# Unsplit float32 expert weights in column strips of the array, with wider transfers and a reordered gather and scatter

## The chip, the cores and the metric

The kernel runs on one core of a Trainium2 chip. The metric is the device time of one execution in microseconds. The kernel before takes 2220.1 us (median of 3 runs, 2218.81 to 2220.77); a difference of 0.2% is about what a measurement of it can tell from none.

A core has a matrix engine (TensorE, PE in the profile; its stationary operand is loaded by separate instructions, PEld), a vector engine (VectorE, DVE), a scalar engine (ScalarE, ACT), GpSimd (POOL) and a queue engine (SyncE, SP) that here does nothing but issue transfers from the chip's main memory.

## The reference

256 tokens of width 1024 pass through two layers of a three-branch mixer, each followed by a feed-forward part (a dense one in the first layer, a mixture of experts in the second), and then through two attention blocks ("fox" and "dsw"). All of it is float32. The change concerns the mixture of experts:

```python
def _moe(h, router_w, router_b, w1, w3, w2):
    logits = (h @ router_w).astype(f32) + router_b.astype(f32)
    probs = jax.nn.softmax(logits, axis=-1)
    top_p, top_i = lax.top_k(probs, TOP_K)                 # 2 of 8 experts per token
    top_p = top_p / jnp.sum(top_p, axis=-1, keepdims=True)
    combine = jnp.sum(jax.nn.one_hot(top_i, N_EXPERTS) * top_p[..., None], axis=-2)
    out = jnp.zeros_like(h)
    for e in range(N_EXPERTS):
        out = out + combine[..., e:e + 1] * _swiglu(h, w1[e], w3[e], w2[e])
    return out                                             # _swiglu: (silu(h @ w1) * (h @ w3)) @ w2
```

w1 and w3 of an expert are 1024 x 2816, w2 is 2816 x 1024. The eight experts' weights are 8 x 3 x 1024 x 2816 x 4 bytes = 276.8 MB, and each is read once. With the inputs given, the router sends 94, 51, 81, 60, 46, 61, 59 and 60 tokens to the experts 0 to 7.

## The kernel before

**How the order is made.** Nearly all instructions are recorded (`Recorder.add`, which is why the profile gives line 95 for them) and put in order by a list scheduler (`Recorder.flush`): it simulates five engines with estimated durations, and picks for each the ready operation of the highest priority. A transfer counts there with its bytes over 360. A `join()` keeps a group of matmuls together as one operation. Transfers go into tiles of fixed pools (`TAGS`: name, bytes per partition, count), and each is issued on SP in that order, so a transfer waits until its tile's last reader is done, and all behind it wait as well. There are two recorded programs: everything up to the end of the experts, and the two attention blocks. Between them the kernel reads the count of the fullest expert, and runs `experts` a second time if some expert has more places than one pass holds.

**The experts (`moe`, `experts`).** Each token gets a place in its expert's list, of which a pass holds 128. A 0/1 matrix G per pair of experts picks the tokens' rows (the gather, 256 columns for the two experts). The normalised tokens are held as a rounded part and a remainder (`s.th`, `s.tl`) in the type float32r, which the array takes in one pass where float32 takes two at half the column rate; the gathered X therefore also has two parts. A weight arrives as float32 in chunks of 512 columns (`chunk`, tag `raw`, 1 MB: four row tiles of 128 x 512). ScalarE copies each 128 x 1024 piece to float32r (`wh`), VectorE subtracts that from the raw piece (`wl`), and `mm3` multiplies three ways: high x high, high x low, low x high, each with the 128 places as stationary operand and 512 columns of weights streaming. w1 and w3 take 8 row tiles per chunk, and their chunks are 5 x 512 and 256 columns. The product g is transposed in 128 x 128 blocks (`turn`), split as well, and multiplied by w2 (`down`): 22 row tiles of two times 512 columns. Per expert that is 8 x 5 x 2 x 3 + 22 x 2 x 3 = 372 matmuls of 512 columns and 8 x 2 x 3 = 48 of 256.

**The scatter.** After two experts the outputs, times the combine weight and the modulation gate, are split and multiplied by the transposed G: 16 matmuls of 512 columns per pair.

**Names in the rows.** `pa`, `pb`, `pt` are PSUM tiles (3, 4 and 1 banks); `F`, `Y`, `G` hold gathered tokens (printed without their digit), `P` the transposed g, `T` scratch, `E` the 0/1 matrices, `hh` and `hl` parts of activations, `M` two more tiles for split weights.

Of the kernel before, what the change touches and what calls it, by code (L numbers as in the profile page):

```python
# [58 lines left out]
class Recorder:  # L59
# [9 lines left out]
    def reset(s):  # L69
        s.ops, s.hist, s.bias, s.wait, s.joined = [], {}, 0.0, WAIT, None  # L70
# [14 lines left out]
    @contextmanager  # L85
    def join(s):

        s.joined = []
        yield
        s.joined = None  # L90

    def add(s, engine, method, args, kw):
# [81 lines left out]
    def flush(s, hold=()):  # L174
# [70 lines left out]
        while events:  # L245
# [9 lines left out]
            while again:  # L255
                again = False
                for e in engines:
# [94 lines left out]
class Net:  # L352
# [166 lines left out]
    def chunk(s, src, mode, tags=None):  # L519
# [35 lines left out]
        return get  # L555

# [762 lines left out]
    def moe(s):  # L1319
# [60 lines left out]
        s.slots = s.c([128, 128], name="slots")  # L1380
        nc.gpsimd.iota(s.slots, pattern=[[1, 128]], base=0, channel_multiplier=0, allow_small_or_imprecise_dtypes=True)
# [10 lines left out]
        s.raws = itertools.chain(["raw"] * 5 + ["Y4"] * 4 + ["hh", "hl"], itertools.repeat("raw"))  # L1392
        s.wh, s.wl = itertools.cycle(["wh"] * 4 + ["M4"]), itertools.cycle(["wl"] * 4 + ["M4"])
        s.experts(0)
        s.wh, s.wl = itertools.repeat("wh"), itertools.repeat("wl")
# [3 lines left out]
        with s.tc.If(vals[0] > 128):  # L1399
            s.experts(128)  # L1400
        s.nc = s.rec

    def experts(s, base):

        nc, A = s.nc, s.A
        for e in range(8):
            if e % 2 == 0 and e and base == 0:
                s.raws = itertools.chain(["raw"] * 8, ["hh", "hl"], itertools.repeat("raw"))
            if e % 2 == 0:

                G = [s.t([128, 2, 128], "E2", F32R) for _ in range(2)]
                for b in range(2):
                    for i in range(2):
                        pos = s.pos[:, b, e + i:e + i + 1]
                        if base:
                            q = s.t([128, 1], "sa")
                            nc.vector.tensor_scalar(q, pos, float(base), None, ALU.subtract)
                            pos = q
                        nc.vector.tensor_scalar(G[b][:, i], s.slots, pos, s.self[:, b, e + i:e + i + 1],
                                                ALU.is_equal, ALU.mult)  # L1420
                tag = ("Y4",) * 4 if e % 4 == 2 else ("F4", "F4", "G4", "G4")
                X = [s.t([128, 4, 256], z, F32R) for z in tag]
                for k2 in range(0, 8, 2):
                    for i, th in enumerate((s.th, s.tl)):
                        p = s.ps("pa", (128, 2, 256))
                        for k in range(2):
                            f = (k2 + k) * 128
                            for b in range(2):
                                nc.tensor.matmul(p[:, k], th[b][:, f:f + 128], G[b].rearrange("p i t -> p (i t)"),
                                                 start=b == 0, stop=b == 1)  # L1430
                        nc.scalar.activation(X[2 * i + k2 // 4][:, k2 % 4:k2 % 4 + 2], p, AF.Copy)

                GTs, cws = [], []
                for i in range(2):
                    p = s.ps("pt")
                    for b in range(2):
                        nc.tensor.transpose(p[:, b * 128:b * 128 + 128], G[b][:, i].bitcast(F32), s.ident)
                    for b in range(2):
                        nc.tensor.matmul(p[:, 256:264], G[b][:, i].bitcast(F32), s.comb[:, b], start=b == 0, stop=b == 1)
                    GT, cw = s.t([128, 256], "E2", F32R), s.t([128, 1], "sa")  # L1440
                    nc.scalar.activation(GT, p[:, 0:256], AF.Copy)
                    nc.vector.tensor_copy(cw, p[:, 256 + e + i:257 + e + i])
                    GTs.append(GT)
                    cws.append(cw)
            o = e % 2 * 128
            xk = lambda k: (X[k // 4][:, k % 4, o:o + 128], X[2 + k // 4][:, k % 4, o:o + 128])
            GT, cw = GTs[e % 2], cws[e % 2]
            w1, w3, w2 = A["moe_w1"][0, e], A["moe_w3"][0, e], A["moe_w2"][0, e]
            y = [s.ps("pb") for _ in range(2)]

            def turn(c0, C, g):
                kt = C // 128
                p = s.ps("pt", (128, kt, 128))
                for k in range(kt):
                    nc.tensor.transpose(p[:, k], g[:, k * 128:k * 128 + 128], s.ident)
                gh, gl = s.t([128, kt, 128], "P2", F32R), s.t([128, kt, 128], "P2", F32R)
                s.evac_split(p, gh, gl)
                return c0, C, gh, gl

            def down(c0, C, gh, gl):  # L1460
                kt = C // 128
                for n in range(2):
                    w = s.chunk(w2[c0:c0 + C, n * 512:n * 512 + 512], "k")
                    for k in range(kt):
                        mm3(nc, y[n], (gh[:, k], gl[:, k]), w(k, 0, 512), c0 == 0 and k == 0, c0 + C == FF and k == kt - 1)

            last = None
            for c0 in range(0, FF, 512):
                C = min(512, FF - c0)
                pr = []  # L1470
                for i, w in enumerate((w1, w3)):
# [4 lines left out]
                    pr.append(p)  # L1476
                    if i == 0:
                        sg = s.t([128, 512], "T2")
                        nc.scalar.activation(sg[:, 0:C], p[:, 0:C], AF.Silu)
                        if last:  # L1480
                            last = turn(*last)
                g = s.t([128, 512], "T2")
                nc.vector.tensor_tensor(g[:, 0:C], sg[:, 0:C], pr[1][:, 0:C], ALU.mult)
                if last:
                    down(*last)
                last = (c0, C, g)
            down(*turn(*last))
            if e % 2 == 0:
                yh, yl = s.t([128, 2, 1024], "hh", F32R), s.t([128, 2, 1024], "hl", F32R)
            for n in range(2):  # L1490
                sl = slice(n * 512, n * 512 + 512)
                hi, lo = yh[:, e % 2, sl], yl[:, e % 2, sl]
                t = s.t([128, 512], "T2")
                nc.vector.scalar_tensor_tensor(t, y[n], cw, s.mod[1, "g2"][:, sl], ALU.mult, ALU.mult)
                nc.scalar.activation(hi, t, AF.Copy)
                nc.vector.tensor_tensor(lo, t, hi.bitcast(F32), ALU.subtract)
            for b, n in [(b, n) for b in range(2) for n in range(2)] if e % 2 else []:
                sl = slice(n * 512, n * 512 + 512)
                p = s.ps("pa")
                for i, z in enumerate((yh, yl)):  # L1500
                    for j in range(2):
                        nc.tensor.matmul(p, GTs[j][:, b * 128:b * 128 + 128], z[:, j, sl], start=i + j == 0, stop=i + j == 2)
                s.add_x(p, None, b, n)
# [422 lines left out]
```

## Time and profile before

| | us |
|---|---|
| median of 3 runs | 2220.1 |
| profiled execution, its own time | 2216.6 |
| span of its instructions | 2214.5 |
| of it, from the experts' first gather matmul to their last scatter | 806 |

| engine | busy, share of the span |
|---|---|
| PE | 2135.7 us, 96% |
| PEld | 1859.2 us, 84% |
| DVE | 1729.4 us, 78% |
| ACT | 1373.1 us, 62% |

The span is cut into 40 slices of 55 us on the page, and the experts fill slices 17 to 31. A matmul's row gives its start and a modelled length of which the last part overlaps the next one; what a matmul costs in a stream is the distance between starts. A float32 matmul stands in the trace as two records (two passes with their own weight loads), one in float32r as one.

### The profile page before, as it was taken

Reading aid. Unit: us, or ns where it says so; the run is one execution under the profiler, and the core shown is the slowest. Engines: PE = TensorE matmul, PEld = TensorE weight load, DVE = VectorE, ACT = ScalarE, POOL = GpSimd, SP = SyncE. Lnnn points to the kernel's source line nnn. Section 1 sums busy time; section 2 is a strip of 40 time slices with the busy share of each in tenths; the row PEclk is TensorE's granted clock in tenths of the full one; section 3 lists DMA queues with packets and bytes.
Section 4 is the critical chain, followed back from the end, with each engine's and each line's share of the span. In section 5 each row is a group of like instructions: output and inputs, shape, how many; then the busy total and the mean of one; then the engine's idle time right before and its main releaser. Section 6 shows DMA issues by size and latency. Waiting matters only on the chain. (4 is left out here: it accounts for less than half of the span.)

```text
span 2214.5 us, 34037 instructions
## 1 busy us (share of the span) xinstructions
PE 2135.7 (96%) x13006; PEld 1859.2 (84%) x13006; DVE 1729.4 (78%) x2691; ACT 1373.1 (62%) x1915; POOL 170.9 (8%) x254
## 2 busy tenths in 40 slices
PE   4999999999899999999999999999998999999999
PEld 3988997998788998788888888888876887999997
DVE  7788889875699776789898888988897556656564
ACT  2654454343774455777777777877786655556564
POOL 3020001000020000000000000000000111212120
PEclk9999999999999998999999999999999999999999
DMA  9436656976436645699999999999996532443450
GB/s 328 166 139 220 238 210 238 331 278 227 144 133 215 226 164 196 214 329 385 335 338 333 344 343 326 374 335 351 330 383 222 186 115 83 157 151 125 138 167 20
DMA packets 281674, 527.97 MB, mean 238 GB/s; under 512 B 10362, under 2 KB 65872, under 8 KB 281504
## 3 DMA queue, kind: packets, MB, share of 16 engines
q1 hardware_dynamic: 279296, 522.23, 66.9%
q0 software_dynamic: 1696, 2.37, 0.3%
q8 instruction: 104, 1.70, 0.3%
q10 hardware_dynamic: 512, 1.13, 0.1%
q14 instruction: 66, 0.54, 0.1%
HBM read 524.64 MB, written 1.05 MB: 237 GB/s over the span
## 5 line engine op out<-in xcount | busy, mean ns | idle before, releaser
L95 DVE TENSOR_TENSOR wl<-raw,wh 128x1024 fp32r<-128x1024 f32 (+1 forms) x800 | 935.4, 1184 | 251.9 <-ACT wh L95 246.9
L95 ACT ACTIVATE wh<-raw 128x1024 fp32r<-128x1024 f32 (+1 forms) x800 | 817.6, 1032 | 485.9 <-PE pa L95 266.2
L95 PE MATMUL pa<-hh,wh 128*128 128x256 f32 x1072 | 302.4, 287 | 0.0
L95 PE MATMUL pa<-hl,wh 128*128 128x256 f32 (+1 forms) x1072 | 299.3, 285 | 0.0
L95 PE MATMUL pa<-hh,wl 128*128 128x256 f32 x1056 | 296.9, 285 | 0.0
L95 PE MATMUL pa<-wh,hh 128*128 128x256 f32 (+1 forms) x920 | 283.9, 335 | 3.6 <-DVE P L95 1.7
L95 PE MATMUL pa<-wh,hl 128*128 128x256 f32 (+1 forms) x920 | 280.1, 330 | 0.0
L95 PE MATMUL pa<-wl,hh 128*128 128x256 f32 (+1 forms) x920 | 278.2, 328 | 0.7 <-DVE wl L95 0.7
L95 PE MATMUL pa<-wh,Y 128*128 128x512 f32 (+1 forms) x784 | 248.4, 383 | 0.5 <-ACT wh L95 0.5
L95 PEld LDWEIGHTS pa<-hh,wh 128*128 128x128 f32 x1072 | 203.2, 191 | 1.0 <-DVE T L95 0.2
L95 PEld LDWEIGHTS pa<-hl,wh 128*128 128x128 f32 (+1 forms) x1072 | 202.5, 191 | 1.5 <-issue 0.8
L95 PEld LDWEIGHTS pa<-hh,wl 128*128 128x128 f32 x1056 | 200.6, 191 | 2.7 <-issue 2.4
L95 PEld LDWEIGHTS pa<-wh,hh 128*128 128x128 f32 x920 | 169.9, 192 | 19.4 <-issue 3.4
L95 PE MATMUL pb<-wh,P 128*128 128x512 f32 x544 | 181.6, 396 | 3.0 <-ACT P L95 2.1
L95 PEld LDWEIGHTS pa<-wl,hh 128*128 128x128 f32 x920 | 169.8, 192 | 13.1 <-DVE wl L95 1.3
L95 PEld LDWEIGHTS pa<-wh,hl 128*128 128x128 f32 x920 | 169.4, 192 | 13.1 <-DVE hl L95 0.2
L95 PEld LDWEIGHTS pa<-wh,Y 128*128 128x128 f32 x784 | 143.4, 188 | 30.6 <-ACT wh L95 1.3
L95 PE MATMUL pa<-wl,Y 128*128 128x512 f32 (+1 forms) x392 | 148.3, 380 | 0.0
L95 PE MATMUL pa<-wh,F 128*128 128x512 f32 (+1 forms) x376 | 138.0, 379 | 0.0
L95 DVE TENSOR_TENSOR M<-raw,M 128x1024 fp32r<-128x1024 f32 (+1 forms) x109 | 128.8, 1182 | 9.5 <-ACT M L95 9.1
L95 ACT ACTIVATE T<-pa 128x256 f32<-128x256 f32 (+1 forms) x215 | 98.0, 489 | 49.8 <-PE pa L95 44.5
L95 PE MATMUL pa<-wl,F 128*128 128x512 f32 (+1 forms) x344 | 127.9, 375 | 0.0
(372 smaller groups left out, 3589.5 us busy)
## 6 DMA issues: line engine op xcount, KB each, us to landing
raw<-in_moe_w SPq DMA_DIRECT2D x230, 1024.0 KB, 8.1
raw<-in_w_in SPq DMA_DIRECT2D x68, 1024.0 KB, 4.9
raw<-in_w_mod SPq DMA_DIRECT2D x36, 1024.0 KB, 5.4
raw<-in_dsw_w_in SPq DMA_DIRECT2D x72, 512.0 KB, 3.5
raw<-in_ffn_w SPq DMA_DIRECT2D x30, 1024.0 KB, 7.6
raw<-in_moe_w SPq DMA_DIRECT2D x48, 512.0 KB, 4.8
raw<-in_fox_w_in SPq DMA_DIRECT2D x16, 1024.0 KB, 5.5
raw<-in_w_mod SPq DMA_DIRECT2D x24, 512.0 KB, 4.7
```

What stands on the lines that cost most here:

```text
L95: op.fn = lambda: getattr(getattr(s.nc, engine), method)(*args, **kw)
```

## The change

- `experts` no longer splits weights or gathered tokens. The gather sums the two parts of the tokens into float32, and the raw weights stream through the array as float32.
- A pass holds 96 places, as 64 and 32. For each row tile of weights (`strips`), two matmuls with the 64 places as stationary operand write partitions 0 to 63 and 64 to 127 of one bank: each takes half of the tile's columns, and they stand on different columns of the array. Then four matmuls (three for the narrower chunk) with the 32 places do the same in four strips of 256 columns.
- Chunks of w1 and w3 are 1024, 1024 and 768 columns; w2 is taken in rows of 1024 columns (`wide`). A transfer is 1 MB into a `raw` tile, or 512 KB into a `wh` or `wl` tile, which now hold raw weights, and its rows in memory are 4096 or 3072 bytes where they were 2048 or 1024.
- G is laid out in three blocks to match the strips, the gate is kept in strips (`s.g2s`), the scatter comes after each expert, as row halves of the array side by side, and is recorded inside the next expert's first chunk; the combine weight is applied on VectorE at the end. The next pair's gather is recorded inside the second chunk of the expert before.
- The second run of `experts` is replaced by two, for more than 96 and more than 192 places.
- The scheduler counts a transfer with its bytes over 400, and the length of a joined group by the busiest of the 32 x 32 cells of the array that it uses. This holds for the whole program.

```diff
@@ Recorder.add
+        if first is not None:
+            place = lambda z: (z.offset // z.ap[0][0] // 32, (z.offset // z.ap[0][0] + z.ap[0][1] + 31) // 32)
+            cells = [(r, c) for r in range(*place(aps[0])) for c in range(*place(outs[0]))]
+            end = max(s.strips.get(z, 0.0) for z in cells) + op.dur
+            s.strips.update((z, end) for z in cells)
+            op.dur = max(s.strips.values())
...
-            first.dur += op.dur * 0.5
+            first.dur = op.dur
@@ Recorder.flush
-            op.prio = tail + op.dur + (2000 + op.bytes / 360 if op.bytes else 0)
+            op.prio = tail + op.dur + (2000 + op.bytes / 400 if op.bytes else 0)
...
-                        dma_free = max(dma_free, end + 1400) + op.bytes / 360
+                        dma_free = max(dma_free, end + 1400) + op.bytes / 400
@@ Net
+    def wide(s, src):
+        KT, C = src.shape[0] // 128, src.shape[1]
+        at = []
+        while len(at) < KT:
+            k0, tag = len(at), next(s.raws)
+            kt = min(TAGS[tag][0] // 4096, KT - k0)
+            raw = s.t([128, kt, C], tag)
+            s.nc.sync.dma_start(raw, src[k0 * 128:(k0 + kt) * 128].rearrange("(k p) c -> p k c", p=128))
+            at += [raw[:, k] for k in range(kt)]
...
+        return lambda k: at[k]
@@ moe
-        s.raws = itertools.chain(["raw"] * 5 + ["Y4"] * 4 + ["hh", "hl"], itertools.repeat("raw"))
...
+        s.raws = itertools.cycle(("raw", "wh", "wl"))
         s.experts(0)
...
-        with s.tc.If(vals[0] > 128):
-            s.experts(128)
+        for base in (96, 192):
+            with s.tc.If(vals[0] > base):
+                s.experts(base)
@@ experts
+        def strips(pa, pb, xa, xb, w, first, last):
+            n = w.shape[1] // 2
+            with s.rec.join():
+                for i in range(2):
+                    nc.tensor.matmul(pa[64 * i:64 * i + 64, 0:n], xa, w[:, i * n:i * n + n], start=first, stop=last)
+            with s.rec.join():
+                for i in range(n // 128):
+                    nc.tensor.matmul(pb[32 * i:32 * i + 32], xb, w[:, i * 256:i * 256 + 256], start=first, stop=last)
...
+                    for i, th in enumerate((s.th, s.tl)):
+                        for b in range(2):
+                            nc.tensor.matmul(p[:, k], th[b][:, f:f + 128], G[b][:, :, 64:192], start=i + b == 0,
+                                             stop=i + b == 2)
...
+        def scatter(e, GT, ya, yb):
...
+            for b in range(2):
+                ps = [s.ps("pa", (128, 2, 256)) for _ in range(2)]
+                with s.rec.join():
+                    for k, z, n in [(k, z, n) for k in range(3) for z in (yh, yl) for n in range(2)]:
+                        r = slice(64 * n, 64 * n + 64)
+                        p, t, c = (ps[n], GT[0][r, 0], 0) if k == 0 else (ps[n][:, k - 1], GT[1][r, k - 1], 512)
+                        nc.tensor.matmul(p if k else p.rearrange("p q c -> p (q c)"), t[:, b * 128:b * 128 + 128],
+                                         z[r, c:c + (256 if k else 512)], start=k == 0 and z is yh, stop=k == 2 and z is yl)
...
-            for c0 in range(0, FF, 512):
-                C = min(512, FF - c0)
...
-                    wc = s.chunk(w[:, c0:c0 + C], "k")
-                    p = s.ps("pa")
-                    for k in range(8):
-                        mm3(nc, p[:, 0:C], xk(k), wc(k, 0, C), k == 0, k == 7)
...
+            for c0, C in ((0, 1024), (1024, 1024), (2048, 768)):
+                n, m = C // 2, C // 8
+                pa, pb = s.ps("pa"), s.ps("pa", (128, 2, 256))
+                w = s.wide(w1[:, c0:c0 + C])
+                for k in range(8):
+                    strips(pa, pb[:, 0], xa(k), xb(k), w(k), k == 0, k == 7)
...
+                w, pa = s.wide(w3[:, c0:c0 + C]), s.ps("pa")
+                for k in range(8):
+                    strips(pa, pb[:, 1], xa(k), xb(k), w(k), k == 0, k == 7)
...
+            late = e, GT, ya, yb
+        scatter(*late)
```

On PE, in expert 0's first chunk of w1, one piece of weights stands before as three matmuls per row tile, two with its high part and one with its low part (`F4` and `G4` are the two parts of X):

```order
L95 MATMUL pa_1717_1780<-wh_1718_1781,F4_1670_1733 128x512
L95 MATMUL pa_1717_1780<-wl_1719_1782,F4_1670_1733 128x512
L95 MATMUL pa_1717_1780<-wh_1718_1781,G4_1672_1735 128x512
L95 MATMUL pa_1717_1780<-wh_1718_1781,F4_1670_1733 128x512
L95 MATMUL pa_1717_1780<-wl_1719_1782,F4_1670_1733 128x512
L95 MATMUL pa_1717_1780<-wh_1718_1781,G4_1672_1735 128x512
```

With the change a row tile of twice the columns stands there as two matmuls that write 64 partitions and four that write 32, straight from the transferred tiles:

```order
L95 MATMUL pa_1687_1750<-raw_1689_1752,F4_1671_1734 64x512 x2
L95 MATMUL pa_1688_1751<-raw_1689_1752,F4_1671_1734 32x256 x4
L95 MATMUL pa_1687_1750<-raw_1689_1752,F4_1671_1734 64x512 x2
L95 MATMUL pa_1688_1751<-raw_1689_1752,F4_1671_1734 32x256 x4
L95 MATMUL pa_1687_1750<-wh_1690_1753,F4_1671_1734 64x512 x2
L95 MATMUL pa_1688_1751<-wh_1690_1753,F4_1671_1734 32x256 x4
L95 MATMUL pa_1687_1750<-wl_1691_1754,F4_1671_1734 64x512 x2
L95 MATMUL pa_1688_1751<-wl_1691_1754,F4_1671_1734 32x256 x4
```

So the width of what stands on the array changes at nearly every row. In PE's whole order from here to the end of the experts 64-wide and 32-wide strips follow each other 893 times; there are 130 changes between strips and whole-array matmuls (transposes and the gather), and 29 between strips and the scatter's row halves.

SP's queue issues these transfers of expert 0, before:

```order
L95 DMA raw_1790_1853<-in_moe_w1 128x4x512
L95 DMA raw_1791_1854<-in_moe_w1 128x4x512
L95 DMA raw_1805_1868<-in_moe_w3 128x4x512
L95 DMA raw_1806_1869<-in_moe_w3 128x4x512
L95 DMA raw_1817_1880<-in_moe_w2 128x4x512
```

and now, with three kinds of tiles in turn:

```order
L95 DMA raw_1718_1781<-in_moe_w3 128x2x1024
L95 DMA wh_1710_1773<-in_moe_w1 128x1024
L95 DMA wl_1711_1774<-in_moe_w1 128x1024
L95 DMA raw_1721_1784<-in_moe_w3 128x2x1024
L95 DMA wh_1719_1782<-in_moe_w3 128x1024
```

Five `raw`, four `wh` and four `wl` tiles together hold 18 row tiles of 512 KB, 9.4 MB, ahead of the matmuls.

## Rows read from the trace of the kernel before

**Rows 1.** The page: busy time, and DMA's share in 40 slices.
```profile
PE 2135.7 (96%) x13006; PEld 1859.2 (84%) x13006; DVE 1729.4 (78%) x2691; ACT 1373.1 (62%) x1915; POOL 170.9 (8%) x254
DMA  9436656976436645699999999999996532443450
```
**Rows 2.** Stretches: length, busy time (count) by engine, PEclk, DMA share, GB/s.
```profile
890.80:1697.00 806.20, 799.38 (x3776) 653.73 (x3775) 707.13 (x722) 617.60 (x708) 0.00 (x0) 1.00 0.92 331
1000.00:1050.00 50.00, 50.00 (x223) 40.56 (x223) 46.64 (x46) 40.77 (x45) 0.00 (x0) 1.00 1.04 385
0.00:50.00 50.00, 18.11 (x68) 14.47 (x69) 39.31 (x90) 13.49 (x26) 20.29 (x39) 1.00 0.95 342
```
**Rows 3.** Groups of the experts' stretch: busy, mean ns | idle before, releaser.
```profile
L95 DVE TENSOR_TENSOR wl<-raw,wh 128x1024 fp32r<-128x1024 f32 (+1 forms) x428 | 482.8, 1152 | 67.9 <-ACT wh L95 64.7
L95 DVE TENSOR_TENSOR M<-raw,M 128x1024 fp32r<-128x1024 f32 (+1 forms) x107 | 126.3, 1181 | 7.3 <-ACT M L95 7.0
```
**Rows 4.** Waits of SP's queue in that stretch: us in total, times, longest.
```profile
SPq L95 <- DVE wl L95: 522.3, 210, 9.4
```
**Rows 5.** Timeline of PE, 512-column weight matmuls: start, us, name, count.
```profile
1203.18 0.39 PE L95 MATMUL pa<-wl,Y 128*128 128x512 f32 x1
...
1205.28 0.40 PE L95 MATMUL pa<-wl,Y 128*128 128x512 f32 x1
```
**Rows 6.** Timeline of PE, 256-column weight matmuls.
```profile
1676.84 0.28 PE L95 MATMUL pa<-wh,Y 128*128 128x256 f32 x1
...
1678.94 0.28 PE L95 MATMUL pa<-M,Y 128*128 128x256 f32 x1
```
**Rows 7.** Timeline of PEld, the passes of two float32 matmuls of 512 columns.
```profile
785.37 0.19 PEld L95 LDWEIGHTS pa<-macc,ones 128*128 128x128 f32 x1 [0.24 <-issue]
785.80 0.19 PEld L95 LDWEIGHTS pa<-macc,ones 128*128 128x128 f32 x1 [0.24 <-issue]
786.23 0.19 PEld L95 LDWEIGHTS pa<-hh,wh 128*128 128x128 f32 x1 [0.24 <-issue]
```
**Rows 8.** Timeline of PE around float32 matmuls on row halves (64*128), three windows.
```profile
2002.59 0.28 PE L95 MATMUL pa<-wh,hl 128*128 128x256 f32 x1
2002.80 0.92 PE L95 MATMUL pb<-F 64*128 64x256 f32 x8
2003.56 0.39 PE L95 MATMUL pb<-M 64*128 64x128 f32 x4
2003.88 0.40 PE L95 MATMUL pa<-wh,hh 128*128 128x256 f32 x1
2004.11 0.28 PE L95 MATMUL pa<-wl,hh 128*128 128x256 f32 x1
...
2003.12 0.38 PE L95 MATMUL pb<-F 64*128 64x256 f32 x2
```
**Rows 9.** Timeline of PE where the stationary operand narrows to 96 columns.
```profile
1745.50 0.39 PE L95 MATMUL pa<-wh,hl 128*128 128x512 f32 x1
1745.73 0.28 PE L95 MATMUL pa<-hh,Y 128*96 128x256 f32 x1
1745.84 0.28 PE L95 MATMUL pa<-hl,Y 128*96 128x256 f32 x1
```
**Rows 10.** Weight loads there: count, busy us, mean ns, idle before.
```profile
L95 PEld LDWEIGHTS pa<-hh,Y 128*96 128x96 f32 x16 | 2.3, 161 | 0.0
L95 PEld LDWEIGHTS pa<-hl,wh 128*128 128x128 f32 x5 | 1.0, 192 | 0.0
```
**Rows 11.** Timeline of PE, a transpose among others.
```profile
1823.61 0.28 PE L95 MATMUL pb<-ident,E 128*128 128x128 f32 x1
1823.72 0.33 PE L95 MATMUL pb<-P,E 128*128 128x65 f32 x2
```
**Rows 12.** Timeline at the branch between the two recorded programs.
```profile
1700.58 0.70 DVE L95 MEMSET Y<- 128x768 f32 x1 [3.23 <-DVEq L1399]
```

More of the change, by code (lines that the diff above doesn't have):

```diff
@@ L69, in reset @@
     def reset(s):
-        s.ops, s.hist, s.bias, s.wait, s.joined = [], {}, 0.0, WAIT, None
+        s.ops, s.hist, s.bias, s.wait, s.joined, s.strips = [], {}, 0.0, WAIT, None, {}
     def region(s, ap):
@@ L86, in join @@
     def join(s):
-        s.joined = []
+        s.joined, s.strips = [], {}
         yield
@@ L1379, in moe @@
         nc.vector.tensor_copy(cnti, cnt)
-        s.slots = s.c([128, 128], name="slots")
-        nc.gpsimd.iota(s.slots, pattern=[[1, 128]], base=0, channel_multiplier=0, allow_small_or_imprecise_dtypes=True)
+        s.slots = s.t([128, 3, 2, 2, 32], "M4")
+        nc.vector.memset(s.slots, -1.0)
+        for d, p, o in ((s.slots[:, 0], [[0, 2], [1, 64]], 0), (s.slots[:, 1, :, 0], [[0, 2], [1, 32]], 64),
+                        (s.slots[:, 2, :, 1], [[0, 2], [1, 32]], 64)):
+            nc.gpsimd.iota(d.rearrange("p a b c -> p a (b c)") if o == 0 else d, pattern=p, base=o, channel_multiplier=0,
+                           allow_small_or_imprecise_dtypes=True)
+        s.slots = s.slots.rearrange("p a b c d -> p (a b c d)")
+        s.g2s = s.t([128, 768], "M4")
+        for c, n, m in ((0, 2, 512), (512, 4, 256)):
+            for i in range(n):
+                sl = slice(i * 128 // n, (i + 1) * 128 // n)
+                nc.vector.tensor_copy(s.g2s[sl, c:c + m], s.mod[1, "g2"][sl, i * m:(i + 1) * m])
         s.th, s.tl = ([s.t([128, 1024], z, F32R) for z in tags] for tags in (("macc", "G4"), ("F4", "g")))
@@ L1405, in experts @@
         nc, A = s.nc, s.A
-        for e in range(8):
[L1407 to L1447, printed above, removed]
-            w1, w3, w2 = A["moe_w1"][0, e], A["moe_w3"][0, e], A["moe_w2"][0, e]
[L1449 to L1465, printed above, removed]
-            last = None
-            for c0 in range(0, FF, 512):
-                C = min(512, FF - c0)
-                pr = []
-                for i, w in enumerate((w1, w3)):
-                    wc = s.chunk(w[:, c0:c0 + C], "k")
-                    p = s.ps("pa")
-                    for k in range(8):
-                        mm3(nc, p[:, 0:C], xk(k), wc(k, 0, C), k == 0, k == 7)
[L1476 to L1483, printed above, removed]
@@ new lines, in strips, with gather @@
+        def strips(pa, pb, xa, xb, w, first, last):
[6 more added lines that the diff above has]
+                    nc.tensor.matmul(pb[32 * i:32 * i + 32], xb, w[:, i * 256:i * 256 + 256], start=first, stop=last)
+        def gather(e):
+            G = [s.t([128, 2, 384], "G4", F32R) for _ in range(2)]
+            for b in range(2):
+                for i in range(2):
+                    pos = s.pos[:, b, e + i:e + i + 1]
+                    if base:
+                        q = s.t([128, 1], "sa")
+                        nc.vector.tensor_scalar(q, pos, float(base), None, ALU.subtract)
+                        pos = q
+                    nc.vector.tensor_scalar(G[b][:, i], s.slots, pos, s.self[:, b, e + i:e + i + 1],
+                                            ALU.is_equal, ALU.mult)
+            X = [s.t([128, 4, 2, 128], z) for z in (("Y4",) * 2 if e % 4 == 2 else ("F4",) * 2)]
+            for k2 in range(0, 8, 2):
+                p = s.ps("pa", (128, 2, 256))
+                for k in range(2):
+                    f = (k2 + k) * 128
+                    for i, th in enumerate((s.th, s.tl)):
+                        for b in range(2):
+                            nc.tensor.matmul(p[:, k], th[b][:, f:f + 128], G[b][:, :, 64:192], start=i + b == 0,
+                                             stop=i + b == 2)
+                nc.scalar.activation(X[k2 // 4][:, k2 % 4:k2 % 4 + 2].rearrange("p k i t -> p k (i t)"), p, AF.Copy)
+            GTs = [(s.t([128, 1, 256], "E2", F32R), s.t([128, 2, 256], "E2", F32R)) for _ in range(2)]
+            for i in range(2):
+                for j, GT in zip((0, 1), GTs[i]):
+                    p = s.ps("pt", (128, 1 + j, 256))
+                    for k, b in [(k, b) for k in range(1 + j) for b in range(2)]:
+                        nc.tensor.transpose(p[:, k, b * 128:b * 128 + 128],
+                                            G[b][:, i, (j + k) * 128:(j + k) * 128 + 128].bitcast(F32), s.ident)
+                    nc.scalar.activation(GT, p, AF.Copy)
+            return X, GTs
@@ new lines, in scatter @@
+        def scatter(e, GT, ya, yb):
+            yh, yl = s.t([128, 768], "hh", F32R), s.t([128, 768], "hl", F32R)
+            for y, sl in ((ya, slice(0, 512)), (yb, slice(512, 768))):
+                t = s.t([128, sl.stop - sl.start], "T2")
+                nc.vector.tensor_tensor(t, y, s.g2s[:, sl], ALU.mult)
+                nc.scalar.activation(yh[:, sl], t, AF.Copy)
+                nc.vector.tensor_tensor(yl[:, sl], t, yh[:, sl].bitcast(F32), ALU.subtract)
+            for b in range(2):
+                ps = [s.ps("pa", (128, 2, 256)) for _ in range(2)]
[5 more added lines that the diff above has]
+                                         z[r, c:c + (256 if k else 512)], start=k == 0 and z is yh, stop=k == 2 and z is yl)
+                for n, p in enumerate(ps):
+                    x = s.x[b][:, n * 512:n * 512 + 512]
+                    nc.vector.scalar_tensor_tensor(x, p.rearrange("p q c -> p (q c)"), s.comb[:, b, e:e + 1], x, ALU.mult, ALU.add)
@@ new lines, in experts, with turn, down @@
+        pair, late = gather(0), ()
+        for e in range(8):
+            X, GTs = pair
+            xa, xb = (lambda k, o=o, n=n, X=X, i=e % 2: X[k // 4][:, k % 4, i, o:o + n] for o, n in ((0, 64), (64, 32)))
+            GT = GTs[e % 2]
+            w1, w3, w2 = A["moe_w1"][0, e], A["moe_w3"][0, e], A["moe_w2"][0, e]
+            ya, yb = s.ps("pb"), s.ps("pb", (128, 256))
+            def turn(c0, C, ga, gb):
+                ts = []
+                for g, n, m in ((ga, C // 256, 128), (gb, 2, C // 8)):
+                    p, t = s.ps("pt", (128, n, 128)), s.t([128, n, 128], "P2")
+                    for k in range(n):
+                        nc.tensor.transpose(p[:, k, 0:m], g[0:m, k * 128:k * 128 + 128], s.ident[0:m, 0:m])
+                    nc.scalar.activation(t[:, :, 0:m], p[:, :, 0:m], AF.Copy)
+                    ts.append(t)
+                return c0, C, *ts
+            def down(c0, C, ta, tb):
+                w, n = s.wide(w2[c0:c0 + C]), C // 256
+                for k in range(C // 128):
+                    strips(ya, yb, ta[:, k % n, k // n * 64:k // n * 64 + 64], tb[:, k % 2, k // 2 * 32:k // 2 * 32 + 32], w(k),
+                           c0 + k == 0, c0 + C == FF and k == C // 128 - 1)
+            last = None
+            for c0, C in ((0, 1024), (1024, 1024), (2048, 768)):
[4 more added lines that the diff above has]
+                    strips(pa, pb[:, 0], xa(k), xb(k), w(k), k == 0, k == 7)
+                ga, gb = s.t([128, 512], "T2"), s.t([128, 256], "T2")
+                nc.scalar.activation(ga[:, 0:n], pa[:, 0:n], AF.Silu)
+                if last:
+                    last = turn(*last)
+                elif late:
+                    scatter(*late)
+                if c0 == 1024 and e % 2 and e < 7:
+                    pair = gather(e + 1)
+                w, pa = s.wide(w3[:, c0:c0 + C]), s.ps("pa")
+                for k in range(8):
+                    strips(pa, pb[:, 1], xa(k), xb(k), w(k), k == 0, k == 7)
+                nc.vector.tensor_tensor(ga[:, 0:n], ga[:, 0:n], pa[:, 0:n], ALU.mult)
+                nc.scalar.activation(gb[0:m], pb[0:m, 0], AF.Silu)
+                nc.vector.tensor_tensor(gb[0:m], gb[0:m], pb[0:m, 1], ALU.mult)
@@ L1484, in experts @@
                 if last:
                     down(*last)
-                last = (c0, C, g)
+                last = (c0, C, ga, gb)
             down(*turn(*last))
[L1488 to L1503, printed above, removed]
+            late = e, GT, ya, yb
+        scatter(*late)
     def gates(s, w, x, out):
```

5 lines of the change are left out of this document (3 added, 2 removed).

## The prediction

> **What bounds the kernel now.** I read the page's busy shares first, then the stretches, then inside the experts' stretch the groups, the waits and the distances between matmul starts. PE is busy in 96% of the span [rows 1], and in the experts' stretch, 806.2 us long, in 799.4, at a granted clock of 1.00 [rows 2]: 6.8 us of idle time are all that waits of any kind cost PE there. VectorE has 707 us of work in it and ScalarE 618, so both keep up. The transfers' share is 0.92 at 331 GB/s, close to full, but the same row tiles came at 385 GB/s for 50 us on end [rows 2], and SP's queue waits mostly for VectorE's splits to give tiles back (522 us, [rows 4]). So the stretch is set by the work on the array, transfers are second, and the splits, the largest groups of VectorE [rows 3], stand on no path.
>
> What the array does there: nine 512-column matmuls in 2.10 us, 0.2333 each [rows 5]; eighteen of 256 columns in 2.10, 0.1167 each [rows 6]. Eight experts have 8 x 372 = 2976 of the first (694.4 us) and 8 x 48 = 384 of the second (44.8): 739.2 of the 806.2 us are weight matmuls.
>
> **The change part by part.**
>
> *The weight matmuls.* A float32 matmul of 512 columns is two passes, and passes follow each other in 0.43 us [rows 7]; I scale that with the columns: 0.215 for 256, 0.3225 for 384. An expert has 2 x 2 x 8 row tiles of w1 and w3 and 22 of w2 with 1024 columns, and 2 x 8 with 768: 432 and 128 in all. If the strips of a group run side by side, a pair of 64-wide strips costs two passes, 0.86 (or 0.645), and a group of four or three 32-wide strips 0.43. The sum is 432 x 0.86 + 128 x 0.645 + 560 x 0.43 = 694.9 us, 44.3 less than before. That they do run side by side is read from the row halves: the six float32 matmuls of [rows 8] (two of 256 and four of 128 columns by the code; a merged row gives the shape of its first) would take 1.72 us one after the other at the rate of [rows 7], 0.86 in pairs, and the next whole-array matmul starts 1.08 after the first.
>
> *Changes of the array's shape.* This is the price that the trace does not show. Whole-array matmuls of 256 columns start 0.117 apart; at the row halves the step in is 0.21, so 0.09 more, and the first pass takes 0.32 where 0.215 is due, 0.10 more, which is the first weight load that nothing hides. On the way out it is the same again: of the 1.08 us all but 0.86 + 0.10 is some 0.1, and 0.23 stands where 0.12 is due [rows 8]. A change to or from row halves thus costs about 0.2 us: 0.095 of standing still and 0.10 of an exposed load. The other row: where the stationary operand narrows from 128 to 96 columns and all rows stay, the step is 0.23 after a 512-column matmul and 0.11 after a 256-column one, that is, nothing [rows 9]. The 893 changes between 64-wide and 32-wide strips lie between these ends, 0 and 0.2 us each, 0 to 179 us; below nothing they can't be, since both kinds need all rows of the same columns. I take 0 for them, because like [rows 9] they change columns and not rows. For the 159 other changes (130 to and from whole-array matmuls, 29 at the scatter's row halves) I take the 0.095 of [rows 8] without the load, which is shorter here: +15.1 us.
> The row halves show that a change of tiling stops the array for 0.095 us [rows 8]. The Trainium skill (TensorEngine Tiling (Array Packing), Key Properties) goes further than rows of this case: changing the tiling mode, not just the tile, drains the engine. By it the 893 changes would cost what the row halves cost, and the sum would be that of the first rival below.
>
> *The rest of PE.* Transposes of g go from 176 to 136, those of G from 16 to 48; one takes 0.11 [rows 11]: -0.9. The 32 small matmuls with the combine weights go, at most 0.11 each; I take -2. The gather has its 128 matmuls of 256 columns as before. The scatter had 64 matmuls of 512 columns, 14.9 us; now 16 groups each stream 2048 columns on both halves, 4 x 0.2333, again 14.9.
>
> *The splits.* 535 pieces on each of ScalarE and VectorE go, 609 us on VectorE alone [rows 3]. Off the path: 0, and at most the 6.8 us of PE's idle time.
>
> *Transfers.* The same bytes in longer rows. 9.4 of the 276.8 MB are in tiles when the gather starts, so 267.4 MB must come during the stretch: 695 us at 385 GB/s, 782 at the 342 of the start, the slowest full stretch [rows 2]. Against the array's 774 (below) the first is hidden and the second would show by 8 us. I take hidden: the nearer row is that of the same weights.
>
> *The new waits.* In a chunk both halves of `pb` share a bank that is free again only after the last product of VectorE; queued behind are the next chunk's matmuls. PE has eight row tiles of `down` there, 8 x 1.29 us, against about 2 us of ScalarE and VectorE: hidden; uncovered it would be 24 times some 2 us. SP's queue only has its tile names changed; it holds 18 row tiles, 23 us of matmuls.
>
> *The second branch.* The branch cost the engines 3.2 us [rows 12]; there are two now: +3.2. Elsewhere the scheduler's figure of 400 moves single instructions: 0, with 5 us either way.
>
> Sum: 806.2 - 44.3 - 0.9 - 2 + 15.1 = 774.1 for the stretch, -32.1; with the branch -28.9. The profiled execution took 2216.6 us, which gives 2187.7; it lay 3.5 under the median of the runs, so the forecast for a median is **2191**.
>
> **The rivals.**
>
> *Every change of strip width costs as at the row halves (slower).* Standing still 0.095 us, and then the first load: 0.10 for 128 columns, and loads scale with columns (192 ns for 128, 161 for 96, [rows 10]), so 0.05 before 64-wide strips and 0.025 before 32-wide ones. The mean is 0.13, times 893 is 118, and 4 more for loads at the other changes: 2191 + 122 = 2313; with the full 0.2 at all 1052 changes 2386. It decides from 29 us / 893 = 0.03 us a change. For it speak the row halves, the only tiles in this trace that stand beside each other; against it the 96 columns, which cost nothing.
> The page on tiling in the Trainium skill states this case as its rule; no run here shows it for columns yet.
>
> *The transfers become the bound.* At 342 GB/s the stretch is 782 instead of 774: 2199, and some us more where a landing is waited for with no work left. For it: the share is 0.92 already. Against it: 385 GB/s from the same weights with shorter rows.
>
> *Strips do not run side by side in float32.* Then the groups take 432 x 3.44 + 128 x 2.58 = 1816 us instead of 695: 3312. Against it stand the row halves; for it only that no column strips are in the trace.
>
> **How the numbers follow.** The forecast has 0.53, with its own range from 2160 (the idle time goes, and the 159 changes cost nothing) to 2216. The transfers have 0.07, the width changes 0.34, strips in turn 0.04, and 0.02 is left for the order elsewhere. The range runs from 2158 to 2345: it holds the first two cases and the lower part of the third, and leaves out its upper part, the fourth and little below, about 0.2. A measurement of this kernel tells 0.2% (4.4 us) from no change. Faster by more: 0.56, nearly all of the first two; within it: 0.04, small prices per change near 0.03 us; slower: 0.40.
>
> **What would show it.** Right: in the profile after, the 64-wide strips' passes start in pairs 0.43 apart, the 32-wide ones in fours 0.215 apart, and a row tile returns every 1.29 us; PE stays busy in the stretch at a clock of 1.00, DMA's share rises, and VectorE and ScalarE fall to under a third there. The first rival: the first start of each group comes some 0.1 us late and its first pass is longer, a row tile takes 1.5 us or more, and DMA's share falls. The second: PE's rows have idle time ended by DMA. Wrong altogether I would be if the clock fell below 1.00 in the stretch, or if the second pass ran (an expert with over 96 places, against the 94 of the reference).

## The result, and the profile after

The changed kernel takes 2314.2 us (median of 4 runs, 2313.7 to 2316.4) where the one before takes 2219.5 in the same comparison: 1.043 times as long, 95% interval 1.041 to 1.045. The forecast was 2191, faster; the time lies inside its range of 2158 to 2345, but on the other side of no change. The first rival, that each change of strip width costs what the row halves cost, said 2313.

The page of the changed kernel, busy time and the DMA share in 40 slices:

```profile
PE 2236.6 (97%) x16198; PEld 1467.2 (63%) x16198; DVE 1088.4 (47%) x2098; ACT 819.6 (35%) x1347; POOL 173.4 (7%) x256
DMA  8536677884546564887888788888884632544450
```

Stretches of it: length, busy time (count) by engine, PEclk, DMA share, GB/s. The first runs from the experts' first gather matmul to their last scatter:

```profile
889.40:1794.00 904.60, 901.15 (x6967) 263.56 (x6966) 68.01 (x125) 70.20 (x145) 0.00 (x0) 1.00 0.83 297
1000.00:1050.00 50.00, 49.73 (x414) 19.04 (x406) 5.88 (x10) 6.43 (x13) 0.00 (x0) 1.00 0.85 313
```

The whole loss lies in the experts' stretch: 904.6 us for 806.2 [rows 2], 98.4 more. VectorE and ScalarE have next to nothing left in it, 68 and 70 us of 707 and 618. Two things that could have been late are not: the granted clock is 1.00, and the transfers went slower than before, 297 GB/s for 331, and were not waited for. PE is busy in 901 of the 904.6 us, where the forecast's terms add up to 774.1. So time goes by within what counts as busy, and it must be read from the distances between starts.

The timeline of PE in the changed kernel, expert 0's first weights (start, us, name, count; strips of 64 are 128*64, strips of 32 are 128*32; 4 records are a pair in two passes, 8 are a group of four in two passes; a merged row gives the shape of its first, and the one at 1013.97 is a four and two pairs):

```profile
1009.96 0.64 PE L95 MATMUL pa<-wl,F 128*32 128x256 f32 x8
1010.52 1.08 PE L95 MATMUL pa<-raw,F 128*64 128x512 f32 x4
1011.43 1.03 PE L95 MATMUL pa<-wh,F 128*64 128x512 f32 x4
1012.39 0.64 PE L95 MATMUL pa<-raw,F 128*32 128x256 f32 x8
1012.96 1.08 PE L95 MATMUL pa<-wl,F 128*64 128x512 f32 x4
1013.97 2.51 PE L95 MATMUL pa<-raw,F 128*32 128x256 f32 x16
1016.41 0.64 PE L95 MATMUL pa<-wh,F 128*32 128x256 f32 x8
1016.86 0.61 PE L95 MATMUL pa<-wl,F 128*32 128x256 f32 x8
1017.29 1.05 PE L95 MATMUL pa<-raw,F 128*32 128x256 f32 x16
```

Here the scheduler happens to let some groups of one width follow each other, so the same rows show a group with and without a change. A group of four behind another four costs 0.43 us (1016.86 to 1017.29), as forecast. A pair of 64 costs 0.91 when it comes behind a four and another pair follows (1010.52 to 1011.43): 0.86 and 0.05 more. When a four follows it costs 0.96 behind a pair (1011.43 to 1012.39), 0.10 more, and 1.01 behind a four (1012.96 to 1013.97), 0.15 more. A four between two pairs costs 0.57 (1012.39 to 1012.96) instead of 0.43.

Cut to single passes, a row tile of 768 columns, from five short windows of the same timeline:

```profile
1300.74 0.54 PE L95 MATMUL pa<-wh,Y 128*64 128x384 f32 x2
...
1301.11 0.84 PE L95 MATMUL pa<-wh,Y 128*64 128x384 f32 x5
...
1301.53 0.63 PE L95 MATMUL pa<-wh,Y 128*32 128x256 f32 x6
...
1301.77 0.39 PE L95 MATMUL pa<-wh,Y 128*32 128x256 f32 x3
...
1302.10 0.54 PE L95 MATMUL pa<-wl,Y 128*64 128x384 f32 x2
```

A pass of 384 columns is due after 0.32, one of 256 after 0.215. The steps are 0.37 (0.05 more), 0.42 (0.10 of standing still before the narrower strips), 0.24 (0.025 more) and 0.33 (0.11 of standing still before the wider ones). So a change from 64 to 32 costs 0.125 us, one back 0.165, 0.145 in the mean. Times 893 that is 129 us, and the forecast's 774.1 for the stretch becomes 903. The five windows are no exception: over all 893 changes of the stretch the steps exceed those within one width by 129.8 us in sum, 0.145 us each.

The longer first pass is read here as the load of the second pass, which nothing hid. The timeline of PEld at the same place, and then two of its rows at a place where pairs of 64 follow each other, with PE's row there:

```profile
1300.73 0.20 PEld L95 LDWEIGHTS pa<-wh,Y 128*64 128x64 f32 x4 [0.41 <-issue]
1301.53 0.15 PEld L95 LDWEIGHTS pa<-wh,Y 128*32 128x32 f32 x6 [0.60 <-issue]
...
1700.13 0.14 PEld L95 LDWEIGHTS pa<-raw,Y 128*64 128x64 f32 x2 [0.29 <-issue]
1700.56 0.14 PEld L95 LDWEIGHTS pa<-raw,Y 128*64 128x64 f32 x2 [0.28 <-issue]
...
1700.56 1.89 PE L95 MATMUL pa<-raw,Y 128*64 128x512 f32 x8
```

Within one width a load starts one pass ahead of its matmul (1700.13 for 1700.56). Behind a change the loads of both passes stand together, from the start of the first pass on (1300.73).

The waits of PE's weight loads in the experts' stretch of the changed kernel (us in total, times, longest):

```profile
PEld pa L95 <- issue: 347.7, 700, 0.8
...
PEld pa L95 <- DMA wh<-in_moe_w: 11.1, 30, 0.4
```

Most of their idle time ends on nothing that the profile shows ("issue"), and they wait for a DMA never longer than 0.4 us. The largest wait of SP's queue in the same stretch:

```profile
SPq L95 <- PE pa L95: 448.1, 259, 9.7
```

It waited for VectorE's splits before [rows 4]; now it waits for PE to finish with the tiles, so the array sets the pace of the transfers and not they its own.

At the branch between the two recorded programs (the timeline of the changed kernel, idle time before in brackets) VectorE now sits idle for 7.07 us where it sat for 3.23 [rows 12]: 3.8 for the second branch, forecast as 3.2.

```profile
1802.15 0.70 DVE L95 MEMSET Y<- 128x768 f32 x1 [7.07 <-PEq L1433]
```

### The profile page after: what moved, and what is told of

The parts are those of the page before. It is cut to its first block, busy times and chain, and to the rows that moved or that the text cites. A ratio compares the mean times of both kernels' runs of the same rounds, so it can differ in the third digit from the quotient of the medians.

```text
span 2314.6 us, 38749 instructions
## 1 busy us (share of the span) xinstructions
PE 2236.6 (97%) x16198; PEld 1467.2 (63%) x16198; DVE 1088.4 (47%) x2098; ACT 819.6 (35%) x1347; POOL 173.4 (7%) x256
## 5 line engine op out<-in xcount | busy, mean ns | idle before, releaser
L95 DVE TENSOR_TENSOR wl<-raw,wh 128x1024 fp32r<-128x1024 f32 x368 | 448.2, 1222 | 170.4 <-ACT wh L95 168.1
L95 ACT ACTIVATE wh<-raw 128x1024 fp32r<-128x1024 f32 x368 | 389.1, 1061 | 336.4 <-PE pa L95 204.3
L95 DVE TENSOR_TENSOR T<-T,pa 128x512 f32<-128x512 f32 (+3 forms) x59 | 32.9, 558 | 521.3 <-PE pa L95 493.2
L95 ACT ACTIVATE T<-pa 128x256 f32<-128x256 f32 (+2 forms) x215 | 94.7, 472 | 408.6 <-PE pa L95 403.7
L95 ACT ACTIVATE P<-pt 128x512 f32<-128x512 f32 (+3 forms) x48 | 22.3, 464 | 429.3 <-PE pt L95 429.3
L95 PE MATMUL pa<-raw,F 128*32 128x256 f32 (+2 forms) x1088 | 147.1, 456 | 0.3 <-DVE x L95 0.3
L95 PE MATMUL pa<-raw,Y 128*32 128x256 f32 (+2 forms) x1088 | 146.3, 455 | 0.5 <-DVE x L95 0.5
L95 PE MATMUL pb<-raw,P 128*32 128x256 f32 (+1 forms) x1056 | 142.5, 466 | 0.0
L95 PE MATMUL pa<-wh,Y 128*32 128x256 f32 (+3 forms) x704 | 132.4, 443 | 0.5 <-DVE x L95 0.5
L95 DVE SCALAR_TENSOR_TENSOR macc<-raw,cond,macc 128x1024 f32<-128x1024 f32 x77 | 98.7, 1282 | 24.2 <-DMA raw<-in_w_mod 23.6
```

What stands on the lines that cost most here:

```text
L95: op.fn = lambda: getattr(getattr(s.nc, engine), method)(*args, **kw)
```

## The experiments

**Theory 1**: each change of strip width stops the array and exposes the load behind it, some 0.145 us together. **Rivals**: A, transfers; B, float32 strips are slow by themselves; C, the rest of the change (planner's numbers, order). In the first three kernels the matmuls and their data are those of the changed kernel and only their order differs.

**Several row tiles at a time.** The 64-wide pairs of 2, 4 or 8 row tiles are issued together, then their 32-wide fours:

```diff
-        def strips(pa, pb, xa, xb, w, first, last):
+        def strips(pa, pb, rows):
+            for r in range(0, len(rows), 8):       # 2, 4 or 8
+                part = rows[r:r + 8]
...
                 with s.rec.join():
+                    for xa, xb, w, first, last in part:
                         for i in range(2):
                             nc.tensor.matmul(pa[64 * i:64 * i + 64, 0:n], xa, w[:, i * n:i * n + n], start=first, stop=last)
                 with s.rec.join():
+                    for xa, xb, w, first, last in part:
                         for i in range(n // 128):
                             nc.tensor.matmul(pb[32 * i:32 * i + 32], xb, w[:, i * 256:i * 256 + 256], start=first, stop=last)
...
```

Two at a time:

> Two row tiles at a time: the 64-wide pairs of both are issued together, then the 32-wide fours of both. The same matmuls on the same data as the changed kernel; the changes between 64-wide and 32-wide strips fall from 893 to 427, nothing else is meant to move. Theory 1 (each such change stops the array: about 0.10 us standing still and 0.03 to 0.05 us of an exposed load, 0.145 us read from single records): 466 x 0.145 = 67.6 us less, 2314 - 68 = 2246. Rival A (the transfers of the weights set the pace): no change, 2314. Rival B (the passes of float32 strips are themselves slower than 0.43 us): no change, 2314. Rival C (the rest of the change, the planner's numbers and the order of scatter and gather): no change, 2314.

Four at a time:

> Four row tiles at a time: 203 changes of strip width where the changed kernel has 893. Theory 1: 690 x 0.145 = 100 us less, 2214. On a line with the run of two row tiles if the price of one change is a constant. Rivals A, B and C: no change, 2314; with rival A it could even be later, since four weight tiles are held until the 32-wide pass frees them.

Eight at a time:

> Eight row tiles at a time: 81 changes of strip width. Theory 1: 812 x 0.145 = 118 us less, 2196, the matmuls' own time; here the transfers may begin to show, since eight weight tiles are held until the 32-wide pass frees them, and then it is between 2196 and 2230 with waits of PE's loads on DMAs of the weights. Rivals A, B and C: no change, 2314.

| row tiles at a time | changes of strip width | median, us | against before, 95% | saved per change of width |
|---|---|---|---|---|
| 1 (the changed kernel) | 893 | 2314.2 | 1.043 (1.041 to 1.045) | |
| 2 | 427 | 2241.7 | 1.010 (1.009 to 1.012) | 72.5 / 466 = 0.156 |
| 4 | 203 | 2212.8 | 0.997 (0.997 to 0.998) | 101.4 / 690 = 0.147 |
| 8 | 81 | 2198.5 | 0.992 (0.990 to 0.993) | 115.7 / 812 = 0.142 |

The time follows the number of changes nearly on a straight line, at the price read from single passes. The last column also holds what the other changes of shape saved, which fell from 159 to 110 with eight at a time. By the distances between starts alone, the changes of width cost 129.8, 61.1, 29.0 and 11.3 us in these four kernels, 0.145 to 0.140 each. Rivals A, B and C expected 2314 each time and fall as causes of the loss. The stretch with eight at a time, in the columns of the stretches above:

```profile
889.40:1674.50 785.10, 778.37 (x6959) 341.27 (x6958) 69.05 (x123) 69.78 (x144) 0.00 (x0) 1.00 0.89 342
```

It is 785.1 us long: the forecast's 774.1 and 81 x 0.145 = 11.7 give 785.8. That they meet so closely is chance: the 774.1 holds 15.1 for 159 other changes, and 110 of them at 0.095 make the sum 781.2. PE's timeline in that kernel, at a place where the strips narrow and widen again:

```profile
1238.99 1.03 PE L95 MATMUL pb<-wl,P 128*64 128x512 f32 x4
1239.85 1.89 PE L95 MATMUL pb<-raw,P 128*64 128x512 f32 x8
1241.67 0.64 PE L95 MATMUL pb<-wh,P 128*32 128x256 f32 x8
1242.12 0.61 PE L95 MATMUL pb<-wl,P 128*32 128x256 f32 x8
1242.56 1.05 PE L95 MATMUL pb<-raw,P 128*32 128x256 f32 x16
1243.42 0.61 PE L95 MATMUL pb<-wh,P 128*32 128x256 f32 x8
1243.85 0.61 PE L95 MATMUL pb<-wl,P 128*32 128x256 f32 x8
1244.28 1.05 PE L95 MATMUL pb<-raw,P 128*32 128x256 f32 x16
1245.26 0.87 PE L95 MATMUL pa<-wh,Y 128*64 128x384 f32 x4
1245.95 0.49 PE L95 MATMUL pa<-wl,Y 128*64 128x384 f32 x2
```

One pair takes 0.86 (1238.99 to 1239.85); the next two take 1.82 with the change behind them, 0.10 more than 1.72. Fours stand 0.43 or 0.44 apart, the first one 0.45. The last two take 0.98 where 0.86 is due, and the first pair behind them 0.69 instead of 0.645. This kernel beats both, the one before by 0.8%.

**The same width throughout.** The 96 places are three blocks of 32, each in strips of 32 columns, row tile by row tile in the code, with no grouping (gather, gate and scatter are laid out to match; not shown):

```diff
-            with s.rec.join():
-                for i in range(2):
-                    nc.tensor.matmul(pa[64 * i:64 * i + 64, 0:n], xa, w[:, i * n:i * n + n], start=first, stop=last)
...
+            if first:
+                with s.rec.join():
+                    for i in range(w.shape[1] // 256):
+                        nc.tensor.matmul(pa[32 * i:32 * i + 32].rearrange("p j c -> p (j c)"), s.zero[:, 0:32], s.zero,
+                                         start=True, stop=False)
+            for j, p in enumerate((pa[:, 0], pa[:, 1], pb)):
+                with s.rec.join():
+                    for i in range(w.shape[1] // 256):
+                        nc.tensor.matmul(p[32 * i:32 * i + 32], xs[j], w[:, i * 256:i * 256 + 256],
+                                         start=first and j == 2, stop=last and j > 0)
...
```

> The 96 places as three blocks of 32, each in four strips of 32 columns side by side (256 columns each): as many columns streamed as in the changed kernel (0.645 us a row tile of 768 or 0.645 for three blocks of 256 in two passes), but no change of strip width at all. It adds 56 zeroing matmuls that open the two blocks of one bank (0.21 us, 12 us in all), 256-wide scatter matmuls in place of 512-wide ones (about 7 us) and more splits on VectorE and ScalarE, taken as hidden. Theory 1: 893 x 0.145 = 129 us less and 19 us more, about 2204; the changes between strips and the whole array stay. Rivals A and C: 2314 or later. Rival B, in which strips of float32 are slow by themselves: as late as the changed kernel or later, since all passes are now narrow strips.

It took 2237.5 us (1.009 times before, 1.007 to 1.010): 76.7 less than the changed kernel, but 33 more than expected. Its timeline, from the zeroing matmuls of a chunk on:

```profile
1009.76 0.40 PE L95 MATMUL pa<-zero 128*32 128x512 bf16 x4
1009.99 1.04 PE L95 MATMUL pa<-wh,F 128*32 128x256 f32 x16
1010.85 1.04 PE L95 MATMUL pa<-wl,F 128*32 128x256 f32 x16
1011.71 1.90 PE L95 MATMUL pa<-raw,F 128*32 128x256 f32 x32
1013.44 1.04 PE L95 MATMUL pa<-wh,F 128*32 128x256 f32 x16
```

Eight records, one block of a row tile of 1024, take 0.43 us on end (16 in 0.86, 32 in 1.73), over changes of the stationary operand. In the whole stretch, where the code also goes from one PSUM bank to the next, every pass with passes of its width before and behind it takes 0.21 or 0.22 us, all 3269. Rival B is out, and so is the thought that long groups as such, or the switch of banks, made the difference. The missing 33 us are mostly my own slip: a row tile of 768 columns fills only three of four strips, so its three blocks cost 1.29 us where the changed kernel's 0.645 + 0.43 are 1.075: 128 x 0.215 = 27.5 us. By the distances between starts the zeroing took 13.8 us for 12, and the scatter's row halves 30.1 where the changed kernel's 19.7 and 7 were expected; that is 5 more.

**The planner's rate back at 360.**

```diff
-            op.prio = tail + op.dur + (2000 + op.bytes / 400 if op.bytes else 0)
+            op.prio = tail + op.dur + (2000 + op.bytes / 360 if op.bytes else 0)
...
-                        dma_free = max(dma_free, end + 1400) + op.bytes / 400
+                        dma_free = max(dma_free, end + 1400) + op.bytes / 360
```

> The changed kernel with the planner's assumed transfer rate put back from 400 to 360. 912 changes of strip width where it had 893. Theory 1: 19 x 0.145 = 3 us more, 2317, nothing else. Rival C (the planner's numbers are the loss): back towards 2220.

2322.0 us, 8 more than the changed kernel (1.046 times before, 1.045 to 1.048). Rival C is out as far as this number goes, which was not the loss but, if anything, a small gain. At the price above, the 19 further changes are 3 of the 8 us. Between the profiled executions the stretch differs by 4.1 us (908.7 for 904.6): its strips take 1.7 more and the scatter's row halves 3.5. The rest was not followed up. The other new rule of the planner, the length of a joined group, was not run by itself.

**Passes that trade places.** Eight at a time, and every other group has its 32-wide pass first:

```diff
+            narrow_first = s.turns % 2
+            s.turns += 1
+            for narrow in (narrow_first, 1 - narrow_first):
...
```

> As the kernel with eight row tiles at a time, but the two passes trade places from one group to the next (64-wide then 32-wide, then 32-wide then 64-wide), so that two groups that follow each other meet at the same width: 62 changes of strip width for 81, and 158 changes of tile shape in all for 191. Theory 1: 19 x 0.145 = 3 us less by the changes of width alone, 5 us by all changes at the same price: 2194 to 2196 where eight at a time had 2198. A rival in which the gain of grouping came from fewer, longer joined blocks (planning, instructions fetched, semaphores) and not from the changes of width: no change, 2198, since the blocks are as many and as long.

2201.5 us, 0.992 times before (0.990 to 0.994), against 2198.5 and the same ratio without: no gain, and a miss for the time, though 3 us are less than the 0.2% that a measurement tells. Adding up the distances from each start to the next by the shape of the tile, its strips take 711.0 us for 714.7, 3.7 less, as theory 1 has it; but the scatter's row halves take 23.3 for 19.8 and the whole-array matmuls 53.8 for 50.1. One place where it went is a wait of the weight loads in the stretch:

```profile
PEld pa L95 <- DVE x L95: 4.2, 5, 0.9
```

With eight at a time in the fixed order the same wait is:

```profile
PEld pa L95 <- DVE x L95: 0.9, 1, 0.9
```

These are the loads behind the scatter, which wait for VectorE to empty a bank. This run doesn't tell the two theories of grouping apart; the one with a single width did.

**How near the transfers are.** Eight at a time, with most 32-wide passes left out:

```diff
-                    for xa, xb, w, first, last in part:
+                    for xa, xb, w, first, last in (part[0], part[-1]):
                         for i in range(n // 128):
```

> Leaves out part of the computation: of eight row tiles at a time, the 32-wide pass (the places 64 to 95) is done for the first and the last only; all weights are still transferred. This takes about 430 of 560 fours away, 0.43 us each, 185 us of TensorE's time, and shows how fast the transfers can go: the experts' stretch carries 283 MB. If the transfers kept up at any speed: 2198 - 185 = 2013. By the 385 GB/s that is the best 50 us seen so far the stretch can't be under 735 us, where eight at a time has 785: about 2150. If the transfers already bound the kernel with eight at a time: no change, 2198.

2111.1 us (0.951 times before, 0.949 to 0.952); 416 of the 560 fours are gone, not 430. Its stretch, and 100 us inside it:

```profile
889.40:1589.00 699.60, 631.01 (x3822) 245.42 (x3823) 68.50 (x124) 69.83 (x145) 0.00 (x0) 0.95 0.98 383
1100.00:1200.00 100.00, 90.55 (x561) 35.56 (x559) 10.91 (x20) 11.18 (x24) 0.00 (x0) 0.98 1.01 399
```

Now the transfers do bound: the DMA share is 1.01, PE idles in a tenth of the time, and the weights come at 399 GB/s. PE's largest wait in the stretch is one for weights, and its idle time that a DMA ended is 57.6 us in all, where with eight at a time there is none:

```profile
PE pa L95 <- DMA wl<-in_moe_w: 28.6, 11, 7.0
```

The floor of the stretch is thus about 700 us, 85 below eight at a time. My 735 was wrong in the amount and not in the rate: I put 283 MB into the stretch, where the first row above has 383 GB/s over 699.6 us, 268 MB, and 268 MB at 385 GB/s are 696 us. The second rival had no ground in any of the kernels that do the whole work: no wait of PE's loads for a DMA is longer than 0.4 us there.

## Why the prediction was wrong

- **The bound** was read rightly: the array's work sets the stretch, before and after; the splits could go with next to no gain (PE's idle time there went from 6.8 to 3.4 us).
- **The weight matmuls**, 694.9 us: right. Strips of float32 stand side by side, 0.86 and 0.43 us a group wherever no change intervenes, so the third rival (one after the other) falls.
- **The changes of the array's shape: the step that failed.** It took 0 for the 893 changes between 64-wide and 32-wide strips, where the runs show 0.145 us each by the distances between starts (0.142 to 0.156 by the times), 129 us in all. The range from 0 to 0.2 was worked out rightly; the choice in it was not. I went by the narrowing to 96 columns [rows 9] because it too changes columns and not rows. But there one tile still takes the place of one tile, while the row halves [rows 8] were the only rows in which the array is cut into several. The nearer row was that with tiles side by side. The size that the first rival took from them, 0.095 of standing still and a load that scales with its columns, is what the passes show: 0.10 or 0.11, and 0.05 or 0.025. That its sum of 2313 lies 1 us from the result is partly luck: its stretch would be 896 us, and 904.6 were measured.
  The rule of the Trainium skill (TensorEngine Tiling (Array Packing), Key Properties), that a change of the tiling mode and not just of the tile drains the engine, agrees with these runs: 0.10 or 0.11 us of standing still at each change of width, and none where the width stays.
- **The 159 other changes**, +15.1 us: too low. I left out the load behind them as shorter here; it is shorter, but not nothing. In the changed kernel's timeline a transpose alone between strips takes 0.26 us (1042.69 to 1042.95) where 0.11 is due. By the distances between starts these changes cost 25.6 us in sum, 8.8 of it by the longer first passes. What the stretch holds beside the weight matmuls and all changes came to 54 us, for 64 in the forecast; the idle time that went is a third of that. The two errors cancel nearly, and only so do 774.1 and 129 come within 2 us of the 904.6.
- **Transposes, combine matmuls, scatter**: small, and not followed one by one. The scatter's row halves took 19.7 us by the distances between starts, where 14.9 were forecast without the steps in and out.
- **Transfers and new waits**, hidden: right. Of the two rates, the 695 us by 385 GB/s is near what the transfers take where they bind, 699.6 in the last experiment; the 342 GB/s of the start is no limit for the stretch, which ran at 383 there.
- **The second branch**, +3.2: 3.8.
- **The chances.** From 0.03 us a change on the kernel is slower, and the bounds of that price were 0 and 0.2. With the only rows of cut tiles at 0.2, the slower side should have had more than 0.40.

## What to carry to other kernels

In these runs tiles of the array side by side stream at full rate only while the shape of the tile stays: count the changes of shape in the order that PE executes, and group the work by width before you narrow it. When the trace has two rows near an operation that it lacks, choose by what the hardware must do differently (here, cutting the array anew), not by which operand dimension the change is in. And where the bounds of a price, times its count, straddle zero gain, the order that lowers the count is worth writing before the kernel runs.

## What the runs showed of the hardware

- Between 64-wide and 32-wide column strips in float32 the array stands still for 0.10 us on narrowing and 0.11 on widening, and the first pass behind it is longer by 0.025 and 0.05 us, read as a load that nothing hides. Within one width neither shows (0.216 us for 256 columns, 0.429 for 512).
- A change between column strips and whole-array matmuls or row halves costs about as much, 0.16 us in the mean of the changed kernel (25.6 us in all).
- One core took weights at 399 GB/s for 100 us with rows of 4096 and 3072 bytes, where 385 was the best 50 us before.
- With PE idle a tenth of the time, waiting for transfers, the granted clock was 0.95 in the mean of the stretch, so for a part of it at the lower of the two levels (1.2 and 2.4 GHz), where it was 1.00, the upper, with PE busy throughout (the last experiment's rows against those of eight at a time). Whether that cost time there beyond the idle time was not measured.
